# Router comparisons in PSUM, another layout of the left tile pool, and gated products written in w2's row order, in a two-layer encoder kernel

## The chip, the cores and the metric

The kernel runs on one core of one Trainium2 chip. The metric is the device time of one execution in microseconds, from the first to the last instruction and what lies around it, with all inputs in DRAM as float32.

## What is computed

Two encoder layers run over 256 tokens of width 1024. Each has a token mixer and a mixture of experts, and after each of them stands a LayerNorm over a scaled residual. Cut to what matters here:

```
for l in range(DEPTH):                                   # DEPTH = 2
    mix = mixer(h, w_in[l], ..., w_out[l])               # attention, window attention, gated delta rule
    h = layernorm(ALPHA * h + mix, ln1_g[l], ln1_b[l])
    s = sigmoid(h @ w_router)                            # 32 experts, 8 groups of 4
    sel = s + router_bias
    # group score = sum of a group's two best sel; the best group; in it the two best experts
    # comb[token, e] = s of a chosen expert / sum of the two, 0 elsewhere
    y = sum(comb[:, e:e+1] * ((silu(h @ w1[l][e]) * (h @ w3[l][e])) @ w2[l][e]) for e in range(32))
    h = layernorm(ALPHA * h + y, ln2_g[l], ln2_b[l])
```

w1 and w3 are 1024 x 512 and w2 is 512 x 1024 for each expert, so a layer reads 192 slabs of 1 MB for its experts.

## The kernel before

**Layers.** `mixer(l)` runs first, then `moe(l)`. Two pools of SBUF tiles stand against each other: the right one holds a ring of NR = 15 places of 8 KB a partition, the left one is opened anew for each mixer (`open_mixer`) and for each mixture of experts. A tile in a newly opened left pool waits for the last reader or writer of whatever lay in the same bytes before.

**Weights of the experts.** `fetcher(l)` lists the 192 slabs (`todo`) in the order of use and issues them on SP's DMA queue, which is in order: a load that waits for its place holds up all loads behind it. The places are the ring of 15 on the right and NL = 7 on the left (`wl0` to `wl6`), used in turn. One more place on the left, `op`, takes the very first slab of expert 0, and later the results of the experts (`ops`), which `combine` reads for the last time in the last matmuls of the layer. So 23 slabs can lie in SBUF before PE has used any, and the 24th needs the place of the second slab in use.

**Router.** `project` ends the mixer: it projects, forms the residual, and computes logits from the transposed h (`hx`, in the bytes of the tile `gc`) before the norm is applied. `moe` then chooses experts on DVE with tensors of 16 to 256 elements a partition. `s` is the sigmoid, `sel` adds the bias, `hi`, `lo`, `m1`, `ml` and `gs` give the group scores, `d8` and `d4` are all pairwise differences of groups and of experts in a group, `ge` and `loss` count who beats whom, and `both` is the choice. PE turns it into ranks (`rk`), DVE into positions (`pos`) and one-hot matrices `P`, with which PE gathers 64 tokens for each expert (`gather`, line 1448 copies them out of PSUM). Beside this chain ACT and POOL split h into an upper part `hh` (ACT casts) and a remainder `hl` (POOL subtractions), which `gather` multiplies by `P`.

**Experts.** For each expert `up` makes 64 matmuls, ACT the tanh (line 1473), DVE two products into `hid`, PE two transposes (`transpose_hid`), ACT a copy to `hidT`, and `down` 16 matmuls. `expert_step(e)` issues up(e), then combine and transposes of P, then down(e - 1), gathers for a later expert, and only then the transposes of hid(e).

**Between the layers.** Layer 2 begins on SP's queue with the two vectors of the closing LayerNorm, broadcast to 128 partitions into `gains` (lines 1574 and 1575), and behind them stand all its weights of the mixer. ACT and DVE cut the first of these weights (`uh`, `ul`) ahead of the norm's statistics (line 235). `gains` lies 20,640 bytes after the pool's start, and so did the place `op`.

Of the kernel before, what the change touches and what calls it, by code (L numbers as in the profile page):

```python
# [113 lines left out]
def kernel(ctx: ExitStack, tc: tile.TileContext, a: dict, out: bass.AP):  # L114
# [1170 lines left out]
    def moe(l, fetch, slab, reserve):  # L1285
        P, W, X, PT, ops, hid, hidT = {}, {}, {}, {}, {}, {}, {}
# [52 lines left out]
        sm = rt[:, 128:].rearrange("p (a b) -> p a b", a=10)  # L1339
        hi, lo = (sm[:, 2 * i:2 * i + 2].rearrange("p a b -> p (a b)").rearrange("p (x c) -> p x c", c=2)  # L1340
                  for i in range(2))
        m1, ml, gs, ge = (sm[:, 4 + i] for i in range(4))
        r2 = sm[:, 8]
# [287 lines left out]
```

## Time and profile before

| | |
|---|---|
| device time, median of 3 runs | 1470.63 us (1470.15 to 1471.12) |
| the profiled execution's own time | 1470.02 us |
| its span, first to last instruction | 1468.4 us |
| busy share of the span: PE, DVE, ACT, POOL | 91%, 43%, 28%, 18% |
| mean DMA rate over the span | 327 GB/s |
| mean granted clock of PE | 0.972 of full speed |

The span falls into two equal halves of a mixer, a router and 32 experts. All rows below come from the profiled execution; a start in a timeline counts from its first instruction. PE is TensorE's matmuls, DVE VectorE, ACT ScalarE, POOL GpSimd, SP the engine that issues most transfers. A bracket at the end of a timeline row gives the idle time before it and what ended that.

### The profile page before, as it was taken

Reading aid. Unit: us, or ns where it says so; the run is one execution under the profiler, and the core shown is the slowest. Engines: PE = TensorE matmul, PEld = TensorE weight load, DVE = VectorE, ACT = ScalarE, POOL = GpSimd, SP = SyncE. Lnnn points to the kernel's source line nnn. Section 1 sums busy time; section 2 is a strip of 40 time slices with the busy share of each in tenths; the row PEclk is TensorE's granted clock in tenths of the full one; section 3 lists DMA queues with packets and bytes.
Section 4 is the critical chain, followed back from the end, with each engine's and each line's share of the span. In section 5 each row is a group of like instructions: output and inputs, shape, how many; then the busy total and the mean of one; then the engine's idle time right before and its main releaser. Section 6 shows DMA issues by size and latency. Waiting matters only on the chain. (4 is left out here: it accounts for less than half of the span.)

```text
span 1468.4 us, 23692 instructions
## 1 busy us (share of the span) xinstructions
PE 1341.5 (91%) x9708; PEld 893.4 (61%) x9708; DVE 632.3 (43%) x1214; ACT 403.8 (28%) x769; POOL 266.2 (18%) x327
## 2 busy tenths in 40 slices
PE   6889999799998999999678799997999899999986
PEld 5768777555554555555367677774555556555542
DVE  6887667622221222222169875775222212222213
ACT  3445543211111111211134455332211111111111
POOL 4485304300000000000036743033000000000000
PEclk9999999899999999999979899999999999999999
DMA  7535779699999999999655457796999999999995
GB/s 232 168 123 148 226 244 344 233 405 419 419 419 417 419 419 419 419 419 420 266 163 156 138 141 255 242 355 239 407 418 419 418 418 419 420 419 419 419 419 212
DMA packets 114533, 479.89 MB, mean 327 GB/s; under 512 B 25168, under 2 KB 38000, under 8 KB 65520
## 3 DMA queue, kind: packets, MB, share of 16 engines
q1 hardware_dynamic: 112464, 471.85, 82.7%
q0 software_dynamic: 1376, 5.24, 1.0%
q8 instruction: 81, 1.33, 0.4%
q10 hardware_dynamic: 576, 1.18, 0.2%
q14 instruction: 36, 0.29, 0.1%
HBM read 476.40 MB, written 1.84 MB: 326 GB/s over the span
## 5 line engine op out<-in xcount | busy, mean ns | idle before, releaser
L176 PE MATMUL h<-w,h 128*64 128x256 f32 x2016 | 232.7, 387 | 21.7 <-PEq L1382 9.5
L176 PEld LDWEIGHTS h<-w,h 128*64 128x64 f32 x2016 | 144.0, 139 | 100.3 <-issue 16.6
L170 DVE SCALAR_TENSOR_TENSOR hid<-hid,h 128x256 f32<-128x256 f32 x64 | 27.0, 421 | 401.3 <-ACT hid L1473 401.3
L170 DVE SCALAR_TENSOR_TENSOR op<-mo,rt,op 64x512 fp32r<-64x512 f32 x128 | 95.9, 749 | 223.0 <-ACT op L1500 222.0
L1500 ACT ACTIVATE op<-mo,rt 64x512 fp32r<-64x512 f32 x128 | 87.4, 683 | 314.5 <-PE mo L176 275.1
L176 PE MATMUL mo<-w,hidT 128*64 128x512 f32 x720 | 164.3, 595 | 3.5 <-DMA w<-in_w_dram 2.2
L161 POOL TENSOR_TENSOR W<-P,rt 128x128 f32<-128x128 f32 x64 | 24.2, 399 | 785.2 <-PE PT L182 710.3
L1473 ACT ACTIVATE hid<-h 128x256 f32<-128x256 f32 x64 | 24.6, 385 | 402.3 <-PE h L176 402.3
L176 PEld LDWEIGHTS mo<-w,hidT 128*64 128x64 f32 x720 | 50.7, 137 | 89.1 <-issue 77.3
L176 PE MATMUL h<-w,xg 128*64 128x256 f32 x864 | 96.9, 380 | 2.3 <-ACT h L1448 2.3
L176 PE MATMUL h<-wl,h 128*64 128x256 f32 x768 | 86.3, 381 | 2.1 <-ACT h L1448 1.4
L176 PEld LDWEIGHTS h<-w,xg 128*64 128x64 f32 x864 | 61.0, 137 | 33.6 <-ACT h L1448 3.4
L176 PE MATMUL mo<-wl,hidT 128*64 128x512 f32 x304 | 69.8, 597 | 2.5 <-DMA wl<-in_w_dram 2.5
L176 PEld LDWEIGHTS h<-wl,h 128*64 128x64 f32 x768 | 53.9, 137 | 29.9 <-ACT h L1448 2.1
L176 PE MATMUL my<-op,PT 128*128 128x512 f32 x256 | 69.7, 412 | 2.1 <-ACT op L1500 1.4
L176 PE MATMUL xg<-P,hh 128*128 128x256 f32 x256 | 56.4, 303 | 5.8 <-DVE P L161 5.8
L176 PEld LDWEIGHTS my<-op,PT 128*128 128x128 f32 x256 | 45.5, 188 | 25.4 <-issue 11.5
L176 PEld LDWEIGHTS xg<-P,hh 128*128 128x128 f32 x256 | 40.8, 196 | 29.6 <-issue 29.5
L176 PE MATMUL xg<-P,hl 128*128 128x256 f32 x256 | 52.7, 288 | 0.0
L176 PE MATMUL h<-wl,xg 128*64 128x256 f32 x416 | 47.7, 382 | 3.2 <-DMA wl<-in_w_dram 1.6
L176 PEld LDWEIGHTS mo<-wl,hidT 128*64 128x64 f32 x304 | 20.6, 137 | 37.3 <-issue 29.8
L176 PE MATMUL wo<-uh_wo,ym 128*128 128x512 f32 x128 | 41.4, 395 | 0.0
(436 smaller groups left out, 2463.9 us busy)
## 6 DMA issues: line engine op xcount, KB each, us to landing
w<-in_w_dram SPq DMA_DIRECT2D x268, 1024.0 KB, 19.9
wl<-in_w_dram SPq DMA_DIRECT2D x112, 1024.0 KB, 19.9
w_gb<-in_w_in_dram SPq DMA_DIRECT2D x16, 512.0 KB, 3.7
w_gc<-in_w_in_dram SPq DMA_DIRECT2D x16, 512.0 KB, 4.5
w_wo<-in_w_out_dram SPq DMA_DIRECT2D x16, 512.0 KB, 4.8
w_ga<-in_w_in_dram SPq DMA_DIRECT2D x14, 512.0 KB, 4.7
w_cqk<-in_w_in_dram SPq DMA_DIRECT2D x8, 512.0 KB, 3.7
w_aq<-in_w_in_dram SPq DMA_DIRECT2D x8, 512.0 KB, 4.5
```

The lines of the kernel that those rows point to most:

```text
L161: return eng.tensor_tensor(out=o, in0=x, in1=y, op=op).ins
L170: return V.scalar_tensor_tensor(out=o, in0=x, scalar=s, in1=y, op0=op0, op1=op1)
L176: ins = T.matmul(o, l, r, start=start, stop=stop, skip_group_check=True).ins
L1473: A.activation(u, b[:, :256], AF.Tanh, scale=0.5)
L1500: A.activation(hi, src, AF.Copy, scale=w)
```

## The change

**Choice of experts.** The tiles of the choice (`s`, `sel`, `hi`, `lo`, `m1`, `gs`, `d8`, `d4`, `loss`) lie in two PSUM banks, `ch` and `d4`. Where an operation takes two tensors, one comes from PSUM and the other from SBUF, for which `sel` and `gs` are computed twice (`sel2`, `gs2` in the SBUF tile `gate`). The pair sums and maxima become reductions. The positions are made in PSUM too (`first`); `P` reads them there, and ACT copies them to `pos`.

**Left pool.** A pad of 128 bytes comes first, so `hh` covers exactly the bytes of `gc`; before, it took in the last 128 bytes of `mix`, the LayerNorm's vectors that POOL reads last. The places `op` and `wl0` change sides, so that `gains` of the next layer lies on `wl0` and `op` on the mixer's `ym0`. The first slab is loaded as the 19th instead of the 16th. h is split token half by token half instead of column half by column half.

**Products.** tanh goes into a tile of its own, `gate`, and the two products read every second element and write `hid` in halves, which the transposes then read without a stride.

```diff
+FIRST = 18
...
                 stt(m1[:, 3:4], m1[:, 0:1], -1.0, m1[:, 2:3], OP.mult, OP.mult)
-                shifted(1, 0, mix[:, 1], m1)
                 logits(1, 1)
                 folded = scaled(1, m1)
+                shifted(1, 0, mix[:, 1], m1)
...
-        todo.insert(NR, todo.pop(0))
+        todo.insert(FIRST, todo.pop(0))
...
-                j = (i if i < NR else i - 1) % (NR + NL) - NR
-                if i == NR:
+                j = (i if i < FIRST else i - 1) % (NR + NL) - NR
+                if i == FIRST:
                     w = lefts.pop("op", None) or left("op")
...
+               "gate": lambda e: st((128, 256), "gate", f"gate{l}{e}"),
...
+        scope["pad"] = st((128, 32), "pad", f"pad{l}")
         X[2] = st((128, 8, 2, 64), "xg", f"xg{l}2")
         W[0], PT[0], P[0] = (new[n](0) for n in ("W", "PT", "P"))
 
         part_h = lambda n: st((128, 2, 8, 128), n, f"{n}{l}", dt=F32R)
         hs = [part_h("hh")]
-        rt = st((128, 288), "rt", f"rt{l}")
-
-        scratch = [st((128, n), x, f"rs{x}{l}") for x, n in (("hid", 256), ("hidT", 256), ("sc", 128))]
+        rt = st((128, 192), "rt", f"rt{l}")
+        both = st((128, 128), "both", f"both{l}", dt=BF16)[:, :64].rearrange("p (t e) -> p t e", t=2)
+        gate[0], hid[0], hidT[0] = (new[n](0) for n in ("gate", "hid", "hidT"))
         fl = st((128, 1), "fl", f"fl{l}", dt=I32)
-        scope["pad"] = st((128, 128), "pad", f"pad{l}")
-        reserve(("op", 0, 1, 2))
+        reserve((0, "op", 1, 2))
         hs.append(part_h("hl"))
         reserve((3, 4, 5, 6))
...
-        for j in range(2):
-            for t in range(2):
+        for t in range(2):
+            for j in range(2):
                 k = slice(4 * j, 4 * j + 4)
                 split(hs[0][:, t, k], hs[1][:, t, k], hv[:, t, k], G)
...
-        s, sel, loss = (scratch[0][:, 64 * i:64 * i + 64].rearrange("p (t e) -> p t e", t=2) for i in range(3))
-        both = scratch[0][:, 192:224].bitcast(BF16).rearrange("p (t e) -> p t e", t=2)
-        d4 = scratch[1].rearrange("p (g i j) -> p g i j", i=4, j=4)
-        d8 = scratch[2].rearrange("p (t i j) -> p t i j", i=8, j=8)
...
+        ch, d4 = bank("s", f"ch{l}"), bank("s", f"d4{l}")[:, :256].rearrange("p (g i j) -> p g i j", i=4, j=4)
+        s, sel, loss = (ch[:, 64 * i:64 * i + 64].rearrange("p (t e) -> p t e", t=2) for i in range(3))
+        d8 = ch[:, 192:320].rearrange("p (t i j) -> p t i j", i=8, j=8)
+        hi, lo = (ch[:, 320 + 32 * i:352 + 32 * i] for i in range(2))
+        m1, gs = (ch[:, 384 + 16 * i:400 + 16 * i] for i in range(2))
+        sel2 = gate[0][:, :64].rearrange("p (t e) -> p t e", t=2)
+        ml, gs2, ge = (gate[0][:, 64 + 16 * i:80 + 16 * i] for i in range(3))
...
-        tt(V, sel, s, rbias[:, None, :].to_broadcast([128, 2, NE]), OP.add)
+        for o in (sel, sel2):
+            tt(V, o, s, rbias[:, None, :].to_broadcast([128, 2, NE]), OP.add)
...
-        tt(V, hi, gv[:, :, 0::2], gv[:, :, 1::2], OP.max)
-        tt(V, lo, gv[:, :, 0::2], gv[:, :, 1::2], OP.add)
-        tt(V, m1, hi[:, :, 0], hi[:, :, 1], OP.add)
-        tt(V, ml, lo[:, :, 0], lo[:, :, 1], OP.max)
-        tt(V, gs, m1, ml, OP.max)
-        tt(V, d4, *pairs(gv, 4), OP.subtract)
-        tt(V, d8, *pairs(gs.rearrange("p (t g) -> p t g", t=2), 8), OP.subtract)
+        for o, op in ((hi, OP.max), (lo, OP.add)):
+            V.tensor_reduce(out=o, in_=sel2.rearrange("p t (x j) -> p (t x) j", j=2), axis=AX.X, op=op)
+        V.tensor_reduce(out=m1, in_=hi.rearrange("p (x c) -> p x c", c=2), axis=AX.X, op=OP.add)
+        V.tensor_reduce(out=ml, in_=lo.rearrange("p (x c) -> p x c", c=2), axis=AX.X, op=OP.max)
+        for o in (gs, gs2):
+            tt(V, o, m1, ml, OP.max)
...
+        against(d8, by_8(gs), by_8(gs2), 8)
+        against(d4, by_4(sel), by_4(sel2), 4)
...
-        stt(pos, rkv, 1.0, both, OP.add, OP.mult)
+        stt(first, rkv, 1.0, both, OP.add, OP.mult)
...
-            u = hid[e] = hid.get(e) or new["hid"](e)
-            A.activation(u, b[:, :256], AF.Tanh, scale=0.5)
-            stt(u, u, 1.0, b[:, :256], OP.add, OP.mult)
-            scope["last"] = [tt(V, u, u, b[:, 256:], OP.mult)]
+            g, u = (x.get(e) or new[n](e) for n, x in (("gate", gate), ("hid", hid)))
+            hid[e] = u
+            A.activation(g, b[:, :256], AF.Tanh, scale=0.5)
+
+            rows = lambda ap: ap.rearrange("s (p j) -> s j p", j=2)
+            uv = u.rearrange("s (j p) -> s j p", j=2)
+            stt(uv, rows(g), 1.0, rows(b[:, :256]), OP.add, OP.mult)
+            scope["last"] = [tt(V, uv, uv, rows(b[:, 256:]), OP.mult)]
...
-                tp(b[:, j * 128:(j + 1) * 128], hid[e][:, j::2])
+                tp(b[:, j * 128:(j + 1) * 128], hid[e][:, j * 128:(j + 1) * 128])
...
-            select(0)
+            select(0, first)
+            A.copy(pos, first)
...
-        scope["stats"] = [sm[:, t] for t in range(2)]
+        scope["stats"] = [sm[:, 2 + t] for t in range(2)]
```

On DVE, in layer 1's choice of experts (all names with `rs` are SBUF tiles of the choice, `rk` is a PSUM bank, `cst` holds constants), there stood, from the differences of experts to the one-hot matrices:

```order
L161 TENSOR_TENSOR rshidT_2710<-rshid_2709 128x256
L161 TENSOR_TENSOR rt_2708<-rt_2708 128x16 x3
L161 TENSOR_TENSOR rssc_2711<-rt_2708 128x128
L161 TENSOR_TENSOR rssc_2711<-rssc_2711,cst 128x128
L161 TENSOR_TENSOR rshidT_2710<-rshidT_2710,cst 128x256
L1363 TENSOR_REDUCE rt_2708<-rssc_2711 128x16
L1366 TENSOR_REDUCE rshid_2709<-rshidT_2710 128x64
L170 SCALAR_TENSOR_TENSOR rshid_2709<-rshid_2709,rt_2708 128x64
L161 TENSOR_TENSOR rt_2708<-rshid_2709 128x64
L170 SCALAR_TENSOR_TENSOR rt_2708<-rk_2765,rshid_2709 128x64
L1536 TENSOR_REDUCE rt_2708<-rt_2708 128x2
L161 TENSOR_TENSOR P_2706<-rt_2708,cst 128x256 x2
```

and now stands (`ch` and `d` are PSUM banks, `gate` and `both` SBUF tiles):

```order
L162 TENSOR_TENSOR gate_2711<-ch_2750,gate_2711 128x16
L162 TENSOR_TENSOR ch_2750<-ch_2750,gate_2711 128x128
L162 TENSOR_TENSOR d_2751<-ch_2750,gate_2711 128x256
L162 TENSOR_TENSOR ch_2750<-ch_2750,cst 128x128
L162 TENSOR_TENSOR d_2751<-d_2751,cst 128x256
L1371 TENSOR_REDUCE gate_2711<-ch_2750 128x16
L1374 TENSOR_REDUCE ch_2750<-d_2751 128x64
L171 SCALAR_TENSOR_TENSOR both_2710<-ch_2750,gate_2711 128x64
L162 TENSOR_TENSOR rt_2709<-ch_2750,both_2710 128x64
L171 SCALAR_TENSOR_TENSOR rk_2770<-rk_2770,both_2710 128x64
L1548 TENSOR_REDUCE rt_2709<-rt_2709 128x2
L162 TENSOR_TENSOR P_2707<-rk_2770,cst 128x256 x2
```

The differences of groups come first, no row shown has two inputs in SBUF, and P reads the positions in the bank `rk`.

On SP, where the last places before layer 1's experts are filled (`w` is a place of the ring, `wl` one on the left, `wl0op` the first slab), there stood:

```order
L1272 DMA w_2541<-in_w_dram 128x2048
L1272 DMA w_2696<-in_w_dram 128x2048
L1272 DMA wl0op_2714<-in_w_dram 128x2048
L1272 DMA wl_2715<-in_w_dram 128x2048
L1272 DMA wl_2716<-in_w_dram 128x2048
L1272 DMA wl_2717<-in_w_dram 128x2048
```

and now:

```order
L1273 DMA w_2541<-in_w_dram 128x2048
L1273 DMA w_2696<-in_w_dram 128x2048
L1273 DMA wl_2715<-in_w_dram 128x2048
L1273 DMA wl_2717<-in_w_dram 128x2048
L1273 DMA wl_2718<-in_w_dram 128x2048
L1273 DMA wl0op_2716<-in_w_dram 128x2048
```

The first slab's load has moved behind three others.

On SP, at the end of layer 1 (with what each row waits for: `DMAHW` other transfers, `PE` and `DVE` those engines), there stood:

```order
L1272 DMA w_5827<-in_w_dram 128x1024 [waits DMAHW1_49]
L1574 DMA gains_5858<-in_ln_g_dram 128x1024 [waits DMAHW2_49,DVE_49,PE_49]
L1575 DMA gains_5858<-in_ln_b_dram 128x1024 [waits DMAHW3_49]
L275 DMA w_5860<-in_w_in_dram 128x2x512 [waits DMAHW4_49]
```

and now:

```order
L1273 DMA w_5862<-in_w_dram 128x1024 [waits DMAHW1_49]
L1586 DMA gains_5893<-in_ln_g_dram 128x1024 [waits DMAHW2_49,PE_49]
L1587 DMA gains_5893<-in_ln_b_dram 128x1024 [waits DMAHW3_49]
L276 DMA w_5895<-in_w_in_dram 128x2x512 [waits DMAHW4_49,PE_49]
```

The order is the same; the load of `gains` no longer waits for DVE, and its wait for PE is now for a slab on the left, not for the layer's last matmuls.

## Rows read from the trace of the kernel before

**Rows 1.** Busy time by stretch: engines (instructions), PE clock, DMA share, GB/s.

```profile
264.00:287.50 23.50, 15.72 (x105) 9.74 (x105) 16.30 (x40) 7.13 (x12) 11.30 (x11) 0.78 0.47 183
287.50:718.50 431.00, 413.31 (x2965) 240.92 (x2966) 100.58 (x198) 72.40 (x154) 10.57 (x28) 0.99 1.00 412
718.50:742.60 24.10, 6.67 (x26) 3.01 (x26) 10.15 (x13) 7.11 (x9) 5.74 (x7) 0.78 0.52 176
```

**Rows 2.** Timeline of SP's DMA issues: start, time, line, destination, count.

```profile
287.51 29.39 SPq L1272 DMA_DIRECT2D w<-in_w_dram  x15
691.72 10.26 SPq L1272 DMA_DIRECT2D w<-in_w_dram  x5
726.89 0.33 SPq L1574 DMA_DIRECT2D gains<-in_ln_g_dram  x1
1016.04 29.39 SPq L1272 DMA_DIRECT2D w<-in_w_dram  x15
```

**Rows 3.** PE timeline, layer 1, first gather, first slabs, second gather, first transposes.

```profile
278.75 0.89 PE L176 MATMUL xg<-P,hh 128*128 128x256 f32 x2 [2.92 <-DVE P L161]
...
282.98 2.75 PE L176 MATMUL h<-wl0op,h 128*64 128x256 f32 x16
...
287.39 0.51 PE L176 MATMUL xg<-P,hh 128*128 128x256 f32 x2
...
289.48 3.67 PE L176 MATMUL h<-w,h 128*64 128x256 f32 x32
294.64 0.48 PE L182 MATMUL hT<-cst,hid 128*128 128x128 f32 x2 [1.49 <-DVE hid L161]
```

**Rows 4.** PE timeline, layer 2, the first gather's first matmuls.

```profile
1008.59 0.89 PE L176 MATMUL xg<-P,hh 128*128 128x256 f32 x2 [2.91 <-DVE P L161]
```

**Rows 5.** DVE timeline, layer 1, router chain; the last row is undisturbed, later.

```profile
268.23 0.33 DVE L165 TENSOR_SCALAR rshid<-lg 128x32 f32<-128x32 f32 x2
...
269.60 1.38 DVE L161 TENSOR_TENSOR rt<-rshid 128x32 f32<-128x32 f32 x2
...
272.26 1.74 DVE L161 TENSOR_TENSOR rshidT<-rshidT,cst 128x256 f32<-128x256 f32 x1
...
275.50 1.44 DVE L161 TENSOR_TENSOR rt<-rshid 128x64 f32<-128x64 f32 x1
276.86 0.21 DVE L170 SCALAR_TENSOR_TENSOR rt<-rk,rshid 128x64 f32<-128x64 f32 x1
...
277.17 1.77 DVE L161 TENSOR_TENSOR P<-rt,cst 128x256 fp32r<-128x256 f32 x2
...
289.93 0.75 DVE L161 TENSOR_TENSOR P<-rt,cst 128x256 fp32r<-128x256 f32 x2
```

**Rows 6.** POOL timeline, layer 1, beside that chain.

```profile
268.22 2.61 POOL L161 TENSOR_TENSOR h<-h,mix 128x512 f32<-128x512 f32 x2 [1.12 <-ACT h L1220]
272.06 6.26 POOL L186 TENSOR_TENSOR hl<-h,hh 128x512 fp32r<-128x512 f32 x4 [1.23 <-DVE rssc L161]
```

**Rows 7.** DVE groups by form, one operand in PSUM: count, busy us, mean ns.

```profile
L170 DVE SCALAR_TENSOR_TENSOR hid<-hid,h 128x256 f32<-128x256 f32 x64 | 27.0, 421 | 401.3 <-ACT hid L1473 401.3
...
L170 DVE SCALAR_TENSOR_TENSOR lg<-lg,stats,bwr 128x32 f32<-128x32 f32 x4 | 1.0, 254 | 0.0
```

**Rows 8.** PE timeline between the layers: last matmuls of layer 1, first after.

```profile
724.64 2.22 PE L176 MATMUL my<-op,PT 128*128 128x512 f32 x7 [0.28 <-DVE op L170]
742.61 1.94 PE L182 MATMUL tp<-cst,h 128*128 128x128 f32 x8 [15.75 <-DVE h L170]
```

**Rows 9.** ACT timeline: a strided cast in layer 1, then the layers' boundary.

```profile
270.86 4.17 ACT L186 CAST hh<-h 128x512 fp32r<-128x512 f32 x4 [2.52 <-POOL h L161]
...
723.12 1.39 ACT L1500 ACTIVATE op<-mo,rt 64x512 fp32r<-64x512 f32 x2 [2.50 <-PE mo L176]
734.27 1.04 ACT L186 CAST uh<-w 128x1024 fp32r<-128x1024 f32 x1 [9.76 <-DMA w<-in_w_in_dram]
```

**Rows 10.** DVE timeline at the boundary: the next layer's first statistics.

```profile
736.60 1.30 DVE L235 BATCH_NORM_STATS2 stats<-my 128x6 f32<-128x512 f32 x2
```

More of the change, by code (lines that the diff above doesn't have):

```diff
@@ L1277, in slab @@
             at[0] += 1
-            while len(got) <= max(i, NR):
+            while len(got) <= max(i, FIRST):
                 fetch(i + 1)
-            return got[NR if i == 0 else i - 1 if i <= NR else i]
+            return got[FIRST if i == 0 else i - 1 if i <= FIRST else i]
         return fetch, slab, lambda js: lefts.update((j, left(j)) for j in js)
     def moe(l, fetch, slab, reserve):
-        P, W, X, PT, ops, hid, hidT = {}, {}, {}, {}, {}, {}, {}
+        P, W, X, PT, ops, gate, hid, hidT = {}, {}, {}, {}, {}, {}, {}, {}
         new = {"P": lambda q: st((128, 2, 4, 64), "P", f"P{l}{q}", dt=F32R),
@@ L1334, in moe @@
         comb, pos = (rt[:, 64 * i:64 * i + 64].rearrange("p (t e) -> p t e", t=2) for i in range(2))
-        s, sel, loss = (scratch[0][:, 64 * i:64 * i + 64].rearrange("p (t e) -> p t e", t=2) for i in range(3))
-        both = scratch[0][:, 192:224].bitcast(BF16).rearrange("p (t e) -> p t e", t=2)
-        d4 = scratch[1].rearrange("p (g i j) -> p g i j", i=4, j=4)
-        d8 = scratch[2].rearrange("p (t i j) -> p t i j", i=8, j=8)
[L1339 to L1343, printed above, removed]
+        ch, d4 = bank("s", f"ch{l}"), bank("s", f"d4{l}")[:, :256].rearrange("p (g i j) -> p g i j", i=4, j=4)
[5 more added lines that the diff above has]
+        ml, gs2, ge = (gate[0][:, 64 + 16 * i:80 + 16 * i] for i in range(3))
+        sm = rt[:, 128:].rearrange("p (a b) -> p a b", a=4)
+        r2, over = sm[:, 0], sm[:, 1, 0:1]
         slotw = r2[:, 12:14]
@@ L1347, in moe, with against @@
         V.reciprocal(s, s)
-        tt(V, sel, s, rbias[:, None, :].to_broadcast([128, 2, NE]), OP.add)
-        gv = sel.rearrange("p t (g c) -> p (t g) c", c=4)
-        pairs = lambda ap, n: (ap[:, :, None, :].to_broadcast([128, ap.shape[1], n, n]),
-                               ap[:, :, :, None].to_broadcast([128, ap.shape[1], n, n]))
-        tie = lambda d, n: C("tie").rearrange("p (i j) -> p i j", j=8)[:, None, :n, :n].to_broadcast([128, d.shape[1], n, n])
-        tt(V, hi, gv[:, :, 0::2], gv[:, :, 1::2], OP.max)
-        tt(V, lo, gv[:, :, 0::2], gv[:, :, 1::2], OP.add)
-        tt(V, m1, hi[:, :, 0], hi[:, :, 1], OP.add)
-        tt(V, ml, lo[:, :, 0], lo[:, :, 1], OP.max)
-        tt(V, gs, m1, ml, OP.max)
-        tt(V, d4, *pairs(gv, 4), OP.subtract)
-        tt(V, d8, *pairs(gs.rearrange("p (t g) -> p t g", t=2), 8), OP.subtract)
+        for o in (sel, sel2):
+            tt(V, o, s, rbias[:, None, :].to_broadcast([128, 2, NE]), OP.add)
+        def against(o, x, y, n):
+            to = [128, o.shape[1], n, n]
+            return tt(V, o, x[:, :, None, :].to_broadcast(to), y[:, :, :, None].to_broadcast(to), OP.subtract)
+        tie = lambda d, n: C("tie").rearrange("p (i j) -> p i j", j=8)[:, None, :n, :n].to_broadcast([128, d.shape[1], n, n])
+        for o, op in ((hi, OP.max), (lo, OP.add)):
[4 more added lines that the diff above has]
+            tt(V, o, m1, ml, OP.max)
+        by_4, by_8 = (lambda ap: ap.rearrange("p t (g c) -> p (t g) c", c=4)), (lambda ap: ap.rearrange("p (t g) -> p t g", t=2))
+        against(d8, by_8(gs), by_8(gs2), 8)
+        against(d4, by_4(sel), by_4(sel2), 4)
         beaten = tt(V, d8, d8, tie(d8, 8), OP.is_ge)
-        V.tensor_reduce(out=ge.rearrange("p (t g) -> p t g", t=2), in_=d8, axis=AX.X, op=OP.max)
+        V.tensor_reduce(out=by_8(ge), in_=d8, axis=AX.X, op=OP.max)
         with tc.issue_after(beaten):
@@ L1374, in moe @@
         ranked = mm(b[:, 64:96], ones, both[:, 1], False, True)
-        rkv = b[:, 0:64].rearrange("p (t e) -> p t e", t=2)
-        stt(pos, rkv, 1.0, both, OP.add, OP.mult)
+        rkv, first = (b[:, i:i + 64].rearrange("p (t e) -> p t e", t=2) for i in (0, 96))
+        stt(first, rkv, 1.0, both, OP.add, OP.mult)
         pin.__exit__(None, None, None)
@@ L1385, in general @@
                 u = st((128, 256), "hid", f"ou{l}")
-                over = sm[:, 9, 0:1]
                 with tc.For_i(0, NE) as e:
@@ L1415, in general, with select @@
                                    part("w2", 8 * half + i), False, False)
-        def select(q):
+        def select(q, pos=pos):
             P[q] = P.get(q) or new["P"](q)
```

## The prediction

> **What bounds the kernel now.** I read the busy time by stretch first. In the 431 us of layer 1's experts the DMA share is 1.00 at 412 GB/s; around it lie two short stretches in which neither PE nor the DMA engines are full: 264.0 to 287.5 us (DMA 0.47, PE busy 15.7 of 23.5 us, clock 0.78) and 718.5 to 742.6 us (DMA 0.52, PE 6.7 of 24.1 us) [rows 1]. A change on DVE or ACT inside the 431 us is worth nothing while the transfers are the limit; the stretches around it are worth their full length.
>
> SP's issues show why the first stretch counts. The 24th slab is issued at 287.51 us in layer 1 and at 1016.04 us in layer 2 [rows 2], when PE has finished the second slab. From there on each slab follows the one before at the DMA rate, and PE keeps up; so whatever makes PE finish the second slab earlier moves the end of the layer by the same amount. PE's rows go back from there: two slabs from 282.98, the first gather from 278.75, and that gather had waited for P on DVE [rows 3]. Layer 2 has the same wait, gathering from 1008.59 [rows 4].
>
> The second stretch is the boundary of the layers. PE's last matmuls end at 724.64 + 2.22 = 726.86, and the next begin at 742.61, 15.75 us later, after the norm [rows 8]. SP issues the norm's `gains` only at 726.89, and the mixer's weights stand behind it in the queue [rows 2]. ACT's first cast of these weights waits for the transfer until 734.27 [rows 9], and the statistics of the norm, behind DVE's part of that cut, start at 736.60 [rows 10], 9.7 us after PE was done with the numbers they read.
>
> **Boundary: the place of `gains`.** Now its load waits for a slab on the left that was read some twenty slabs earlier, no longer for the layer's last matmuls. It can be issued behind the last experts' slabs: five go out from 691.72 on in 10.26 us [rows 2], the last at about 702 and 2.5 us apart, so at that step the first six loads of layer 2 are in the queue by about 717. What is late next is ACT, which finishes the last results at 723.12 + 1.39 = 724.51 [rows 9]; the cast can then follow at once if the weight is there. From cast to statistics took 736.60 - 734.27 = 2.33 us [rows 9, 10], so the statistics start at 726.84, just as PE ends: 9.7 us gained. The doubt is the landing. Before, the weight was usable 734.27 - 726.89 = 7.4 us after the first issue [rows 2, 9]. If the whole 7.4 us began only at 718.5, where the experts' stretch ends, the cast would start at 725.9 and the gain would be 8.4. As the transfers overlap the last slabs I take nearer the upper end, **9.4 us**. POOL's and DVE's cuts of the other first weights shift with it, and so does every later load, since each waits for a cut.
>
> **Router chain, twice.** DVE's chain starts at 268.23 and P begins at 277.17 and ends at 278.94 [rows 5]. POOL works beside it from 268.22 to 270.83 and from 272.06 to 278.32 [rows 6]. DVE operations with two inputs in SBUF are stretched there: the 128x256 comparison takes 1.74 us, the 128x64 product 1.44, the two P 1.77, where two P without POOL beside them take 0.75 [rows 5]. The position step, with one input in PSUM, takes 0.21 in the middle of POOL's run [rows 5]. So one input in PSUM escapes the wait. Operations with one PSUM operand cost 0.25 us for 32 elements and 0.42 for 256 [rows 7].
>
> The new chain up to the choice has 18 operations. It starts 0.2 us later, at 268.45, since the norm's `shifted` now stands ahead. I cost it so: the two first ones 0.33 together [rows 5], and by these two prices (0.25 at 16 to 64 elements, 0.42 at 256, the line between for 128) ten small ones at 0.2 to 0.25, two of 128 at 0.3, two of 256 at 0.42 and two counting reductions at 0.3 and 0.4, together 4.9, and 0.5 for the steps between them. It ends near 273.9, where the old one ended near 275.5 with the 1.44 us product following it [rows 5]. The bounds: 0.8 us better if the small ones are as short as the 0.21 row and the steps overlap, and no gain in this part if each of the 18 costs 0.1 more because of PSUM. Behind it stand the ranks on PE (an estimate of 0.5, with the weighted choice on DVE beside them, no longer 1.44), the positions (0.21), a sum (0.2) and two P at 0.42 each [rows 5, 7]. P ends at about 275.7, against 278.94: **3.2 us** earlier.
>
> Three things hang on it. `hl`: the first gather now needs POOL's third subtraction, since the halves go token by token. But `hh` no longer waits for POOL's last read of `mix`, so ACT can start at about 268.4, not 270.86 [rows 9], and POOL at 270.9, not 272.06; at 6.26 / 4 = 1.57 us each [rows 6] the third ends at 275.6, level with P. No cost, but POOL would be next if DVE were faster. Second, the copy of the positions on ACT: ACT is free from about 273 to the first gather's copy, so nothing. Third, the first slab's later load: it is the 19th of 23, and the DMA share of 0.47 [rows 1] says that all 23 have landed after some 11 of the 23.5 us, so nothing; if it came last it would still be there.
>
> **Strided products.** 64 pairs of products of 0.42 us each [rows 7] now read every second element. ACT's strided cast of 512 elements takes 4.17 / 4 = 1.04 us, as much as a contiguous one of 1024 [rows 9]. The price thus lies between nothing and a doubling, 0.84 us for a pair. It is covered by `down` of the expert before, which stands between up and the transposes, except for expert 0, where PE waited 1.49 us for hid [rows 3]. I take 0.3 us for each layer. Contiguous reads in the transposes gain nothing that a DMA-bound stretch could show.
>
> The Trainium skill, page "SBUF — State Buffer", section "Door 1: The DMA port swizzle", says that accesses that leave a line of 16 bytes (8 in PSUM) pay a penalty, so that the stride costs most for the operand in PSUM. No row here shows a product with that stride; with a full doubling by that rule the sum would be 1.1 us worse, an estimate.
>
> The Trainium skill's page "VectorE: DVE Perf Modes", section "Why PSUM operands drop a tier", speaks against the move itself: a PSUM operand keeps float32 at one element a cycle, while single-input operations in SBUF may run at two. By it the few single-input steps of the chain would lose at most 0.3 us in a layer, an estimate, and the sum would be 0.6 us worse.
>
> **The clock.** PE's granted clock averages 0.78 in 264 to 287.5 us [rows 1]; at its lower level the first gather with the two transposes of W behind it took 282.98 - 278.75 = 4.2 us, where the second gather, without such transposes, took 2.1 [rows 3]: the factor between 1.2 and 2.4 GHz. PE still idles over 3 us ahead of the gather, so I let the clock fall as before. The second slab ended 8.8 us after the gather's start in layer 1 and 7.5 in layer 2 [rows 2 to 4]; I keep the sum of the two.
>
> **Sum.** 9.4 + 2 x (3.2 - 0.3) = 15.2 us. The profiled execution took 1470.02 us, so 1454.8; the median of the runs is 0.6 above it: **1455.4 us**, 1.0% faster. Differences under 0.2% (2.9 us) are about what a measurement of this kernel cannot tell from no change.
>
> **Rivals.**
> - *The boundary alone gains.* PSUM writes make the chain as long as it was, or POOL's `hl` comes later and the gather waits for it. Then 9.4 - 0.6 = 8.8 us, 1461.8. For it: no row shows a chain of DVE operations from PSUM to PSUM. Against it: the stretched rows alone hold 1.0 + 1.2 + 1.3 us of waiting [rows 5].
> - *The clock stays up in the gather.* With the idle time halved, PE gathers at 2.4 GHz: 2.1 us, 0.4 for the transposes and 3.67 for two slabs [rows 3], 6.2 in place of 8.8 and 7.5. That is 3.9 us more in all, 1451.5. Against it: 3 us of idle time remain.
> - *The router alone gains.* Loads of layer 2 land late, because they share the DMA engines with the last slabs and hold those up: the boundary gains only 2 to 4 us, 1461 to 1463.
> - *Slower.* The strided products outgrow their cover. Between up(e) and the transposes of hid(e) lie 16 matmuls with the columns of 32 of `up`, which take 3.67 us [rows 3]; a tanh as long as a product needs 0.4 of that. The pair would have to take more than 3.25 us, nearly four times 0.84, before PE waited, and then each 0.1 us costs up to 6.2 us over 62 experts; from 3.5 us on the kernel is slower than before, with a pair of 3.6 us about 1477. The nearest strided row shows a factor of two.
> - *The change does not reach the path*, because another wait (the flag, the copy of the positions) ends where P ended: within 0.2%, 1470.
>
> Chances: the forecast (1453 to 1459) 0.58, boundary alone 0.15, clock up 0.14, router alone 0.07, no effect 0.03, slower 0.03. The range from 1450 to 1462 takes in the first three. Faster 0.94, same 0.03, slower 0.03.
>
> **What would show it.** SP's issue of `gains` at about 705 us instead of 726.89; ACT's cast near 722 to 725 in time, right behind the last results; the statistics less than 1 us after PE's last matmul. P ending some 7.3 us after the chain's start instead of 10.7, no DVE row of the choice above 0.6 us, the next slab issued about 3 us earlier against the logits in each layer. The experts' stretches keep 431 us at full DMA share. Wrong would be a gather that starts after P and behind POOL, a PSUM row at twice its price, or a boundary where ACT still waits for a transfer.

## The result, and the profile after

The changed kernel takes 1453.11 us (median of 4 runs, 1452.09 to 1454.18) against 1470.63: a ratio of 0.9878 (95% interval 0.9864 to 0.9891), 1.2% faster. The forecast was 1455.4, in a range from 1450 to 1462. The profiled execution took 1453.74 us, span 1452.1 us; before it was 1470.02 and 1468.4.

Busy time by stretch of the changed kernel, with the same columns and bounds moved along, answers to [rows 1]:

```profile
264.00:283.10 19.10, 15.02 (x91) 9.41 (x88) 12.72 (x41) 7.27 (x13) 11.02 (x11) 0.82 0.57 222
283.10:715.00 431.90, 412.15 (x2965) 240.17 (x2966) 100.54 (x198) 72.30 (x153) 10.57 (x28) 0.99 1.01 414
715.00:729.50 14.50, 6.76 (x27) 3.02 (x26) 10.10 (x13) 7.17 (x9) 5.74 (x7) 0.93 0.62 215
```

The two short stretches shrank, 23.5 to 19.1 us and 24.1 to 14.5; between them lies the stretch at full DMA share, nearly as long as before (431.9 us, 431.0 then). SP's queue shows the same two gains (answer to [rows 2]):

```profile
283.13 29.26 SPq L1273 DMA_DIRECT2D w<-in_w_dram  x15
...
702.21 0.33 SPq L1586 DMA_DIRECT2D gains<-in_ln_g_dram  x1
...
709.69 5.33 SPq L276 DMA_DIRECT2D w_ga<-in_w_in_dram  x3
...
999.78 29.27 SPq L1273 DMA_DIRECT2D w<-in_w_dram  x15
```

The 24th slab goes out at 283.13 in place of 287.51, in layer 2 at 999.78 in place of 1016.04, and the gains at 702.21 in place of 726.89, with the loads of layer 2 behind them.

PE's timeline around the first gather (answer to [rows 3, 4]); the last column is idle time before a row and what ended it:

```profile
274.32 0.88 PE L177 MATMUL xg<-P,hh 128*128 128x256 f32 x2 [0.94 <-DVE P L162]
275.00 0.63 PE L177 MATMUL xg<-P,hl 128*128 128x256 f32 x2
...
277.99 0.63 PE L183 MATMUL PT<-cst,W 128*128 128x128 f32 x2
278.55 2.81 PE L177 MATMUL h<-wl0op,h 128*64 128x256 f32 x16
281.19 1.89 PE L177 MATMUL h<-w,h 128*64 128x256 f32 x16
...
283.36 0.40 PE L177 MATMUL xg<-P,hl 128*128 128x256 f32 x2
```

The gather starts at 274.32 and still waits for P. Its first row takes 0.88 us and those behind it 0.63 us for two matmuls, where the second gather takes 0.40: it runs at the lower clock, as before. DVE's chain, which answers to [rows 5]:

```profile
267.64 0.50 DVE L166 TENSOR_SCALAR ch<-lg 128x32 f32<-128x32 f32 x2
268.17 0.56 DVE L1350 RECIPROCAL ch<-ch 128x64 f32<-128x64 f32 x1
...
270.28 0.18 DVE L162 TENSOR_TENSOR ch<-ch,gate 128x16 f32<-128x16 f32 x1
270.50 0.17 DVE L162 TENSOR_TENSOR gate<-ch,gate 128x16 f32<-128x16 f32 x1
270.70 0.30 DVE L162 TENSOR_TENSOR ch<-ch,gate 128x128 f32<-128x128 f32 x1
271.04 0.43 DVE L162 TENSOR_TENSOR d<-ch,gate 128x256 f32<-128x256 f32 x1
...
271.71 0.42 DVE L162 TENSOR_TENSOR d<-d,cst 128x256 f32<-128x256 f32 x1
...
272.82 0.22 DVE L171 SCALAR_TENSOR_TENSOR both<-ch,gate 128x64 bf16<-128x64 f32 x1
...
273.75 0.76 DVE L162 TENSOR_TENSOR P<-rk,cst 128x256 fp32r<-128x256 f32 x2
...
274.61 1.58 DVE L162 TENSOR_TENSOR rt<-rt 128x64 f32<-128x64 f32 x1
```

Nothing in it takes more than 0.56 us up to P. The comparison of 128x256 elements fell from 1.74 to 0.42 us and the two P from 1.77 to 0.76 us. One row is long, the product at 274.61 (1.58 us): its two inputs lie in SBUF, and POOL is still running. POOL and ACT beside it (answers to [rows 6, 9]):

```profile
267.53 2.68 POOL L162 TENSOR_TENSOR h<-h,mix 128x512 f32<-128x512 f32 x2 [1.12 <-ACT lg L1184]
270.16 5.95 POOL L187 TENSOR_TENSOR hl<-h,hh 128x512 fp32r<-128x512 f32 x4
```

```profile
267.43 2.15 ACT L187 CAST hh<-h 128x512 fp32r<-128x512 f32 x2
```

ACT's first two casts `hh` no longer wait for POOL at 267.43, and POOL's third `hl` ends at 270.16 + 3/4 x 5.95 = 274.62, 0.11 us after P's end (274.51). Last the boundary: PE, ACT and DVE (answers to [rows 8 to 10]):

```profile
721.29 2.22 PE L177 MATMUL my<-op,PT 128*128 128x512 f32 x7 [0.29 <-DVE op L171]
729.55 1.94 PE L183 MATMUL tp<-cst,h 128*128 128x128 f32 x8 [6.04 <-DVE h L171]
```

```profile
719.77 1.39 ACT L1511 ACTIVATE op<-mo,rt 64x512 fp32r<-64x512 f32 x2 [2.50 <-PE mo L177]
721.22 1.05 ACT L187 CAST uh<-w 128x1024 fp32r<-128x1024 f32 x1
```

```profile
722.30 1.22 DVE L187 TENSOR_TENSOR ul<-w,uh 128x1024 fp32r<-128x1024 f32 x1 [0.28 <-ACT uh L187]
723.55 1.29 DVE L236 BATCH_NORM_STATS2 stats<-my 128x6 f32<-128x512 f32 x2
...
726.58 3.48 DVE L171 SCALAR_TENSOR_TENSOR h<-h,stats,gains 128x512 f32<-128x512 f32 x2
```

The cast of layer 2's first weights starts 0.06 us after ACT's last results end (719.77 + 1.39 = 721.16), and the statistics at 723.55, 0.04 us after PE's last matmul (721.29 + 2.22 = 723.51). PE idles 6.04 us in place of 15.75.

### The profile page after: what moved, and what is told of

Same layout as the page of the kernel before. It is cut to its first block, busy times and chain, and to the rows that moved or that the text cites. A ratio compares the mean times of both kernels' runs of the same rounds, so it can differ in the third digit from the quotient of the medians.

```text
span 1452.1 us, 23761 instructions
## 1 busy us (share of the span) xinstructions
PE 1340.0 (92%) x9708; PEld 892.1 (61%) x9708; DVE 626.2 (43%) x1218; ACT 404.1 (28%) x771; POOL 263.9 (18%) x327
## 5 line engine op out<-in xcount | busy, mean ns | idle before, releaser
L171 DVE SCALAR_TENSOR_TENSOR hid<-gate,h 128x256 f32<-128x256 f32 x64 | 26.9, 421 | 405.3 <-ACT gate L1481 405.3
L1481 ACT ACTIVATE gate<-h 128x256 f32<-128x256 f32 x64 | 24.5, 384 | 406.3 <-PE h L177 406.3
```

Of the source, the lines that this page charges most:

```text
L171: return V.scalar_tensor_tensor(out=o, in0=x, scalar=s, in1=y, op0=op0, op1=op1)
L1481: A.activation(g, b[:, :256], AF.Tanh, scale=0.5)
```

## The experiments

Each kernel ran in turns with the kernel before, the first four of the table on one chip, the next four on a second, the last four on a third. The kernel before had medians of 1469.75, 1468.86 and 1469.65 us there. after_again is the changed kernel once more. The times:

| kernel | median us | ratio to the kernel before, 95% interval |
|---|---|---|
| boundary_alone | 1461.33 | 0.9942 (0.9928 to 0.9955) |
| router_alone | 1462.05 | 0.9951 (0.9937 to 0.9964) |
| choice_in_sbuf | 1461.18 | 0.9947 (0.9933 to 0.9960) |
| pe_kept_busy | 1450.94 | 0.9876 (0.9861 to 0.9891) |
| after_again | 1453.25 | 0.9889 (0.9872 to 0.9905) |
| pe_kept_busy_full | 1450.15 | 0.9872 (0.9855 to 0.9888) |
| hh_over_mix | 1455.56 | 0.9905 (0.9888 to 0.9921) |
| old_product_order | 1452.95 | 0.9891 (0.9875 to 0.9908) |
| boundary_filled | 1452.09 | 0.9882 (0.9866 to 0.9899) |
| pe_busy_transposes_later | 1448.84 | 0.9859 (0.9839 to 0.9880) |
| all_three | 1449.11 | 0.9863 (0.9846 to 0.9879) |
| first_fifteen | 1451.88 | 0.9879 (0.9862 to 0.9895) |

Whole times differ by a microsecond or two between executions of one kernel: layer 1's mixer, the same code in all of them, ends between 266.0 and 267.9 us. So I read three distances inside each trace. The first is from the start of PE's last logits row (`lg<-gap`) to that of the first gather row (`xg<-P,hh`), for the router's chain. The second is from there to SP's issue of the 24th slab (for after, 283.13 - 274.32 = 8.81). The third is from PE's last `my` to the first `tp` between the layers. All in us, layer 1 / layer 2:

| kernel | logits to gather | gather to 24th slab | between the layers |
|---|---|---|---|
| before | 11.69 / 11.70 | 8.76 / 7.45 | 15.75 |
| after | 7.95 / 7.96 | 8.81 / 8.94 | 6.04 |
| after_again | 7.98 / 7.96 | 8.36 / 8.89 | 6.05 |
| boundary_alone | 11.68 / 11.69 | 8.72 / 8.83 | 6.03 |
| router_alone | 7.98 / 7.96 | 8.41 / 7.44 | 15.78 |
| choice_in_sbuf | 12.42 / 12.41 | 7.90 / 8.24 | 6.06 |
| hh_over_mix | 7.96 / 7.96 | 9.54 / 9.48 | 6.03 |
| old_product_order | 7.96 / 7.97 | 8.72 / 7.36 | 6.06 |
| pe_kept_busy | 7.97 / 7.96 | 7.07 / 7.07 | 6.05 |
| pe_kept_busy_full | 7.96 / 7.97 | 7.06 / 7.07 | 6.05 |
| boundary_filled | 7.97 / 7.96 | 8.31 / 7.56 | 5.95 |
| pe_busy_transposes_later | 7.96 / 7.96 | 6.46 / 6.43 | 6.05 |
| all_three | 7.95 / 7.96 | 6.43 / 6.43 | 5.98 |
| first_fifteen | 7.96 / 7.96 | 7.61 / 8.73 | 6.07 |

### The two parts apart

boundary_alone is the kernel before with this edit and the index `FIRST` in the fetcher; router_alone is the changed kernel with both lines set back:

```diff
+FIRST = 18
-        reserve(("op", 0, 1, 2))
+        reserve((0, "op", 1, 2))
```

> Kernel before, with only the places on the left and the step of the first slab's load taken from the change. Theory (the two parts of the change add up, since a transfer-bound stretch lies between them): the statistics of the norm between the layers start as PE's last matmul ends, 9.7 us earlier, the router's chain stays as it was: 1470.6 - 9.7 = 1460.9 us. Rival (the boundary's gain is partly given back by the loads that now share the DMA engines with the last slabs, and the router's part brought more): 1463 to 1465. Rival (most of the 17.5 us came from the boundary): 1456 or less.

> Changed kernel, with the left places and the first slab's load as in the kernel before. Theory: SP issues the gains only when PE is done, the statistics start 9.7 us later than in the changed kernel, and the router's part stays: 1453.1 + 9.7 = 1462.8 us. Rival (the router's shorter chain is worth little, the slabs are held back by the transfers anyway): 1468 to 1470. With the run of the boundary alone: the two gains should sum to 17.5 us; a sum well above or below says that one part gives something back to the other.

The boundary alone brings 1469.75 - 1461.33 = 8.4 us, the router alone 7.7 us, together 16.1; the whole change brought 17.5 beside one set of runs and 15.6 beside another (after_again). The distances separate cleanly: boundary_alone has the short boundary and the long chain, router_alone the reverse. The 8.4 is less than the 9.7 between PE's rows at the boundary: in boundary_alone's profile the two stretches from the gather to the 24th slab took 1.3 us more than in the profile of before, though the edit doesn't touch their code. PE's rows between the layers in router_alone:

```profile
720.21 2.21 PE L177 MATMUL my<-op,PT 128*128 128x512 f32 x7 [0.29 <-DVE op L171]
738.20 1.94 PE L183 MATMUL tp<-cst,h 128*128 128x128 f32 x8 [15.78 <-DVE h L171]
```

So the parts add up, and neither hangs on the other. The "router worth little" and "most of it from the boundary" rivals are out.

first_fifteen keeps the new places and sets only the step of the load back (`FIRST = 15`):

> Changed kernel, with the first slab's load at the 16th step again, the places on the left as in the changed kernel. Theory (the place of gains brings the gain between the layers, not the step of the load): the first slab's load now waits for the place that lies between that of gains and the units, it may be issued some microseconds later, but all slabs have landed long before the first gather: within 1 us of 1453.2. Rival (the order of the loads matters, since the slabs behind it in the queue are issued later): 1 to 3 us slower.

1451.88 us, and the boundary is 6.07 us. SP issues the first slab's load at 251.84 in place of 254.57, the last of the eight on the left goes out at about 266 us in both, and from its issue to its first use the slab has 27 us with this edit and 24 in the changed kernel. The place brings the boundary's gain; the step of the load brings nothing that shows.

### The place of the choice: PSUM or SBUF

```diff
-        ch, d4 = bank("s", f"ch{l}"), bank("s", f"d4{l}")[:, :256].rearrange("p (g i j) -> p g i j", i=4, j=4)
-        s, sel, loss = (ch[:, 64 * i:64 * i + 64].rearrange("p (t e) -> p t e", t=2) for i in range(3))
-        d8 = ch[:, 192:320].rearrange("p (t i j) -> p t i j", i=8, j=8)
-        hi, lo = (ch[:, 320 + 32 * i:352 + 32 * i] for i in range(2))
-        m1, gs = (ch[:, 384 + 16 * i:400 + 16 * i] for i in range(2))
+        d4 = hidT[0].rearrange("p a b -> p (a b)").rearrange("p (g i j) -> p g i j", i=4, j=4)
+        s, sel = (hid[0][:, 64 * i:64 * i + 64].rearrange("p (t e) -> p t e", t=2) for i in range(2))
+        loss = gate[0][:, 112:176].rearrange("p (t e) -> p t e", t=2)
+        d8 = hid[0][:, 128:256].rearrange("p (t i j) -> p t i j", i=8, j=8)
+        hi, lo = (gate[0][:, 112 + 32 * i:144 + 32 * i] for i in range(2))
+        m1, gs = (gate[0][:, 176 + 16 * i:192 + 16 * i] for i in range(2))
```

> Changed kernel, with the tiles of the choice of experts in SBUF in place of PSUM; the same operations in the same order, and the places of hh, of hl and of the slabs unchanged. Theory (operations with two inputs in SBUF wait for POOL's running instruction): several rows of the chain grow from 0.2-0.4 us to 1.0-1.8 us, the first gather starts 2.5 to 3.5 us later in each layer: 1458 to 1460 us. Rival (the chain became shorter through hh's earlier start and the rebuilt steps, not through the place of its tiles): rows stay below 0.6 us, 1453 to 1454.

It took 1461.18 us: the router's whole gain is gone and a little more. DVE's rows, the same operations, though the differences of experts (`hidT<-hid,gate`) now come ahead of those of groups:

```profile
267.68 0.28 DVE L166 TENSOR_SCALAR hid<-lg 128x32 f32<-128x32 f32 x2
...
269.51 1.01 DVE L162 TENSOR_TENSOR hidT<-hid,gate 128x256 f32<-128x256 f32 x1
...
270.66 1.38 DVE L162 TENSOR_TENSOR gate<-gate 128x16 f32<-128x16 f32 x2
272.07 1.50 DVE L162 TENSOR_TENSOR hid<-gate 128x128 f32<-128x128 f32 x1
273.60 1.48 DVE L162 TENSOR_TENSOR hid<-hid,cst 128x128 f32<-128x128 f32 x1
275.00 1.73 DVE L162 TENSOR_TENSOR hidT<-hidT,cst 128x256 f32<-128x256 f32 x1
```

Two operations on 16 elements took 1.38 us together; they took 0.18 and 0.17 in PSUM. The 128-element steps took 1.50 and 1.48 (0.30), the 256-element ones 1.01 and 1.73 (0.43 and 0.42). POOL was at work beside all of these rows, from 270.21 to 276.45 us with its four `hl`, 1.56 us each here (1.49 in the changed kernel). After that, at 279.12, the 64-element product `rt<-rt` with both inputs in SBUF took 0.22 us, where it took 1.58 beside POOL in the changed kernel. Steps with one input went the other way: the nine of the choice take 2.65 us in the changed kernel and 2.19 here, the first two 0.50 and 0.28. The first gather came 4.46 us later against the logits, more than the 2.5 to 3.5 I had put down, because I had counted the rows that were stretched before and not the small ones that the rebuilt chain adds. So the move into PSUM carries the router's gain; the earlier `hh` and the rebuilt steps without it lost 0.7 us (12.42 against 11.69). The two other reorderings, the cut of h by token halves and the norm's `shifted` ahead of the choice, were not run alone. The Trainium skill, page "SBUF — State Buffer", section "Who interferes with whom", says that a VectorE instruction with two SBUF inputs contends with a GpSimd instruction that reads SBUF, and that one with at most one SBUF input, outside the modes that use two ports, does not. The rows here agree: 1.38 us against 0.35 for the same pair of steps.

### POOL's `hl`: how near it is to the path

The 128 bytes ahead of `X[2]` and `hh` go behind them:

```diff
-        scope["pad"] = st((128, 32), "pad", f"pad{l}")
...
         fl = st((128, 1), "fl", f"fl{l}", dt=I32)
+        scope["pad"] = st((128, 32), "pad", f"pad{l}")
```

> Changed kernel, with hh moved down by 128 bytes on the left, so that it overlaps the end of mix again as in the kernel before. Theory (the free start of hh keeps POOL's hl off the path): ACT's first hh starts only when POOL has read mix, 2.7 us later, POOL's third hl ends 1.1 us later, behind P, and the first gather's matmuls on hl wait for it: 0.7 to 1.1 us a layer, 1.5 to 2.2 us in all. Rival (POOL's cut has more than a microsecond of slack, since the gather begins with hh): no change.

1455.56 us, 2.3 above the changed kernel on the same chip. ACT, POOL and PE:

```profile
270.99 4.19 ACT L187 CAST hh<-h 128x512 fp32r<-128x512 f32 x4 [2.69 <-POOL h L162]
```

```profile
272.19 5.97 POOL L187 TENSOR_TENSOR hl<-h,hh 128x512 fp32r<-128x512 f32 x4 [1.23 <-ACT hh L187]
```

```profile
275.09 0.88 PE L177 MATMUL xg<-P,hh 128*128 128x256 f32 x2 [0.94 <-DVE P L162]
...
276.71 0.58 PE L177 MATMUL xg<-P,hl 128*128 128x256 f32 x1 [0.52 <-POOL hl L187]
```

The gather still starts 7.96 us after the logits, but its matmul on `hl` for the second half of the tokens waits 0.52 us for POOL. The next matmuls on `hh` start 1.99 us after the gather's start (277.08) in place of 1.11 (275.43 in the changed kernel), 0.88 later, within the 0.7 to 1.1 expected, and the 24th slab is issued 9.5 us after the gather's start in both layers. So the early start of `hh`, which hangs on 128 bytes of padding, is part of the gain: without it the faster chain runs into POOL's cut.

### The order of the gated products

```diff
-            stt(uv, rows(g), 1.0, rows(b[:, :256]), OP.add, OP.mult)
-            scope["last"] = [tt(V, uv, uv, rows(b[:, 256:]), OP.mult)]
+            stt(u, g, 1.0, b[:, :256], OP.add, OP.mult)
+            scope["last"] = [tt(V, u, u, b[:, 256:], OP.mult)]
-                tp(b[:, j * 128:(j + 1) * 128], hid[e][:, j * 128:(j + 1) * 128])
+                tp(b[:, j * 128:(j + 1) * 128], hid[e][:, j::2])
```

> Changed kernel, with the gated products written in the order of their columns again and the transposes reading every second element, as in the kernel before. Theory (a stride of two elements costs DVE nothing here): the two products stay at 0.42 us each, PE's wait for hid at expert 0 stays near 1.5 us, the transposes of hid take up to 0.07 us more each, all of it hidden by the transfers: within 1 us of the changed kernel. Rival (the estimate on record, 0.3 us a layer for the stride): the products are shorter by 0.1 to 0.4 us, the time 0.6 us lower.

1452.95 against 1453.25 us. DVE's groups by form, count, busy us and mean ns, first of the changed kernel, then of this one:

```profile
L171 DVE SCALAR_TENSOR_TENSOR hid<-gate,h 128x256 f32<-128x256 f32 x64 | 26.9, 421 | 405.3 <-ACT gate L1481 405.3
L162 DVE TENSOR_TENSOR hid<-hid,h 128x256 f32<-128x256 f32 x64 | 26.9, 420 | 2.2
```

```profile
L171 DVE SCALAR_TENSOR_TENSOR hid<-gate,h 128x256 f32<-128x256 f32 x64 | 27.0, 421 | 406.3 <-ACT gate L1481 406.3
L162 DVE TENSOR_TENSOR hid<-hid,h 128x256 f32<-128x256 f32 x64 | 26.9, 420 | 2.2
```

421 and 420 ns with the stride and without it. In the changed kernel the first product reads both its inputs at a step of two elements, the second one its input in PSUM; the outputs are written without a step. That stride cost nothing here, so the 0.3 us a layer put down for it was not there.

### The clock in the gather

Two kernels fill PE's idle time ahead of the gather by repeating starts, the matmuls that put h into the sums `yb`. The edit shown is that of pe_kept_busy_full, with three whole starts; in pe_kept_busy the first and the last of the three are matmuls of 256 columns (`mm(yb[0][0][:, :256], ident, h[:, 0, :256], True, False)`):

```diff
             start(1, 0)
+            start(0, 0)
             start(1, 1)
+            start(1, 1)
...
+        start(1, 1)
         stt(first, rkv, 1.0, both, OP.add, OP.mult)
```

> Changed kernel, with four more matmuls in each layer that repeat the start of the sums yb in PE's idle time ahead of the first gather (they write the same numbers once more). Theory (the granted clock falls because PE idles 1.7 and 0.9 us ahead of the gather): the first gather and the two transposes run at 2.4 GHz, the second slab ends 6.3 us after the gather's start in place of 8.8 and 8.9, 5.1 us in two layers: 1448 us. Rival (the clock is down for another reason than these idle times): the rows of the gather stay at 0.63 us for two matmuls, 1453, or up to 1 us more where a repeated start stands ahead of the ranks.

> The changed kernel itself, unaltered, so that the runs beside it have it on the same chip: 1452 to 1453 us, ratio to the kernel before 0.987 to 0.989.

> Changed kernel, with three more matmuls of 512 columns in each layer that repeat whole starts of the sums yb in PE's idle time ahead of the first gather; the result is unaffected. Theory (idle time ahead of the gather lets the granted clock fall): the gather's matmuls take 0.40 us for two in place of 0.63, the second slab ends 7.1 us after the gather's start as in the run with half starts, in place of 8.8 and 8.9; W on POOL is what PE waits for next; 3.5 us less than the changed kernel in the same call. Rival (what the run with half starts gained is given back elsewhere, or was the difference between two executions): within 1 us of the changed kernel.

The half starts do change the sums `yb` after all, so that kernel's time counts for the placing of the matmuls alone. The whole starts leave `yb` as it is: 1450.15 us, all four runs (1448.97 to 1451.52) below those of the changed kernel beside them (1451.72 to 1453.86), and 1.30 and 1.82 us less from the gather to the 24th slab. Stretches with the granted clock, ahead of the gather and in it, first of the changed kernel, then with the whole starts:

```profile
268.00:274.30 6.30, 2.83 (x11) 0.94 (x10) 5.68 (x22) 3.74 (x4) 6.22 (x5) 0.94 1.00 421
274.30:278.50 4.20, 4.18 (x18) 3.88 (x18) 2.84 (x8) 0.58 (x2) 2.57 (x4) 0.50 0.23 98
```

```profile
268.00:274.70 6.70, 5.84 (x18) 2.08 (x16) 5.97 (x24) 4.16 (x4) 6.62 (x5) 1.00 1.00 422
274.70:278.00 3.30, 2.90 (x19) 2.31 (x18) 2.93 (x8) 0.79 (x3) 2.67 (x4) 1.00 0.30 124
```

A granted clock of 0.50 is 1.2 GHz, 1.00 is 2.4. With PE busy 5.84 us ahead of the gather in place of 2.83 it does not fall there. What PE waits for next is POOL's W:

```profile
274.73 0.69 PE L177 MATMUL xg<-P,hh 128*128 128x256 f32 x2
275.26 0.40 PE L177 MATMUL xg<-P,hl 128*128 128x256 f32 x2
...
277.46 0.68 PE L183 MATMUL PT<-cst,W 128*128 128x128 f32 x2 [0.37 <-POOL W L162]
278.08 1.95 PE L177 MATMUL h<-wl0op,h 128*64 128x256 f32 x16
```

That wait and the two transposes go behind the second slab in the next kernel:

```diff
-            transpose_P(0)
...
                     gather(0, 6)
+                    transpose_P(0)
```

> The kernel with PE kept busy ahead of the gather (1450.15 us), with the two transposes of W for the first pair of experts moved behind the second slab. Theory (they and PE's wait for W on POOL, 0.4 + 0.6 us, lie on the path to the second slab's end, on which SP's next load hangs): the second slab ends about 0.6 to 1.0 us earlier against the gather's start, 6.1 to 6.5 us in place of 7.1; 1448 to 1449 us. Rival (the first slab now waits for the gather's last copies on DVE and ACT for as long as the transposes took): no change, 1450.

The 24th slab goes out 6.43 to 6.46 us after the gather's start, 0.6 earlier in each layer; a wait of 0.41 us for the gather's last copy on DVE took back the rest. 1448.84 us is 1.3 us below the 1450.15 on the other chip, which the spread of the runs (1446.83 to 1451.6) does not settle.

### The clock between the layers

```diff
+            if l == 0:
+                b = bank("s", f"idle{l}")
+                for _ in range(12):
+                    mm(b[:, :256], ident, cst[:, :256], True, True)
```

> Changed kernel, with twelve matmuls of 256 columns on constants in PE's 6.0 us of idle time between the layers; nothing reads what they write. Theory (the idle time lets the granted clock fall for the first 4.6 us of layer 2): the eight transposes of the norm's result take about 1.0 us in place of 1.94 and the first ga matmuls 0.39 in place of 0.63 for one, up to 2.3 us less: 1451 us. Rival (PE there waits for the cuts of the weights, so that a faster PE only idles more): the rows of PE are shorter and the time is within 1 us of 1453.2.

> Changed kernel, with PE kept busy ahead of the gather in both layers, PE kept busy between the layers, and the first transposes of W behind the second slab. Theory: the three gains add, 3.1 + 2 + 1.5: 1446 to 1447 us, faster than both kernels. Rival (what the clock gives at the boundary is lost in the mixer, which is held by the cuts and not by PE): 1448 to 1449.

PE between the layers in boundary_filled:

```profile
721.60 5.34 PE L177 MATMUL idle<-cst 128*128 128x256 f32 x24
727.71 1.32 PE L183 MATMUL tp<-cst,h 128*128 128x128 f32 x8 [0.77 <-DVE h L171]
...
731.14 0.40 PE L177 MATMUL ga<-uh_ga,placeT 128*128 128x512 f32 x1
```

The clock stays at 1.00 (0.56 in the changed kernel from 729.5 to 735) and the rows are shorter: the second set of transposes starts 735.24 - 727.71 = 7.53 us after the first, in the changed kernel 738.27 - 729.55 = 8.72 (8.13 to 9.14 in all kernels with its boundary and no fill). From there the lead is lost: from the first `tp` to layer 2's last logits row it is 253.39 us, 253.33 in the changed kernel. In all_three it is 251.28, but from 252.38 to 253.99 in the kernels that have the changed kernel's boundary. The times say no more: 1452.09 against 1453.11 and 1453.25 on other chips and 1451.88 on the same chip (first_fifteen, the changed kernel but for the step of one load), and all_three at 1449.11 against 1448.84 without this fill. Whether the fill is worth up to a microsecond or nothing stays open. All four runs of all_three (1447.38 to 1450.04) and three of the four of pe_busy_transposes_later (1446.83 to 1449.27, the fourth 1451.6) lie below those of first_fifteen (1451.54 to 1452.62); which of the two is better these runs don't tell.

## Why the prediction was right, point by point

The median came out 2.3 us below the forecast of 1455.4, at the lower edge of the 1453 to 1459 that the forecast kept for itself, and nearer to the 1451.5 of the rival in which the clock stays up. The time alone doesn't choose between the two; the gather's rows at 0.63 us do. The medians moved by 17.5 us, and by 15.6 beside after_again, so a microsecond or two belongs to the runs and not to the kernel; the account below is of the two profiled executions.

The profiled spans differ by 1468.4 - 1452.1 = 16.3 us. The traces split it so: boundary 15.75 - 6.04 = 9.7; logits to gather 2 x 3.74 = 7.5; gather to the 24th slab 16.2 - 17.8 = -1.5; and, in stretches that the change doesn't touch, layer 1's mixer 0.7 and layer 2's 1.0 faster, layer 1's transfer-bound stretch (24th slab to the last `my`'s end, 439.35 and 440.38) 1.0 slower. That sums to 16.3. The terms of the forecast, 15.2 in all, against these:

- **Boundary, 9.4: it was 9.7.** The loads were in the queue by 715 (709.69 + 5.33, the third of the `w_ga`), and no transfer was waited for at the first cast. The doubt about the landing, 8.4, did not come true.
- **Router chain, 3.2 a layer: it was 3.74.** The chain to the choice took 5.4 us (267.64 to 273.04), as costed (4.9 + 0.5). What was too dear stood behind it: ranks, positions, sum and P took 1.47 us (273.04 to 274.51), where 1.8 were put down, and the chain started 0.1 later, not 0.2. The two P overlap, 0.76 together where 2 x 0.42 was taken. Within the chain two errors cancel: the two first steps took 0.50 where 0.33 from SBUF rows was put down, and the steps lay closer together than the 0.5 allowed. The single-input steps lost 0.46 us to PSUM (2.65 against 2.19 in choice_in_sbuf), where the prediction had weighed at most 0.3. The mechanism, one input in PSUM, is shown by choice_in_sbuf.
- **POOL level with P: so it was,** 274.62 and 274.51, and hh_over_mix shows what it costs to lose that.
- **Strided products, 0.3 a layer: nothing.** By the Trainium skill's page "SBUF — State Buffer", section "Door 1: The DMA port swizzle", which was weighed in the prediction, the stride should have cost most in PSUM (of PSUM the page names only matmuls); here 421 ns stayed 421, and the measurement decides.
- **The clock, kept as before: it fell as before,** but the time it took to come back is no property of the kernel. The prediction read a factor of two from 4.2 and 2.1 us, but the 4.2 hold two transposes more; without them the first gather takes 277.99 - 274.32 = 3.67 us here, 1.75 times the second. The sum over two layers was 16.2 in the profile of before, 17.5 in boundary_alone, which has the same code there, and between 15.85 and 17.75 in the kernels that have the changed code there and no fill. So 1.5 us of the account is the difference of two executions. For the same reason the 24th slab went out 3.7 us earlier against the logits in layer 1 and only 2.2 in layer 2, where about 3 was the sign to look for.

The errors of 0.3, 1.1 and 0.6 us on one side and the clock's 1.5 on the other nearly cancel, which is luck, and the two mixers and the transfers add 0.6. Of the rivals, "the boundary alone gains" fails by router_alone, "the router alone" by boundary_alone, the strided products by the rows above. "The clock stays up" did not happen, and was nevertheless the best lead: made to happen, it gave 3.1 us from the 17.25 that the two stretches take in after_again. The 3.9 forecast for it counts from 16.3, and from there the 14.1 measured are 2.2 (7.07 us to the 24th slab in place of 6.2, with 0.37 of them the wait for W).

## What to carry to other kernels

Where a chain of small VectorE operations runs beside GpSimd on the path, look first at whether both inputs lie in SBUF: putting one of them in PSUM took 4.5 us out of 12.4 here (choice_in_sbuf against the changed kernel). A tile's place on the chip is a wait like any other: ask of each early load which tile it overwrites and who reads that last. Where PE waits ahead of a step that decides, look at its granted clock: harmless matmuls in the idle time were worth 3.1 us of 1453 ahead of the gathers, and nothing that shows between the layers. Ahead of the gathers the next engine that was nearly late, POOL with W, took back 0.37 us.

## What the runs showed of the hardware

- Operations from PSUM to PSUM or with one PSUM input cost as little as 0.17 to 0.23 us for 16 to 64 elements and 0.42 to 0.43 for 256, and a step of two float32 elements in the inputs, the one in PSUM among them, added nothing to 420 ns. Steps with one input were shorter from SBUF to SBUF (0.28 us against 0.50 for two of 32 elements).
- Idle times of 0.82, 1.72 and 0.94 us with a few short matmuls between them brought PE to 1.2 GHz; with the idle times filled it stayed at 2.4. When it came back differed between executions whose code is the same in that stretch: 7.36 to 8.94 us from the gather's start to the 24th slab in the kernels with the changed code there and no fill, 7.06 or 7.07 in all four gathers with PE kept busy and nothing else moved.
- At the boundary DVE's two steps on `h` with two inputs in SBUF take 3.48 us beside POOL (726.58), where the same two for the other half of the tokens, with POOL idle, took 1.41 (735.71). That a PSUM input would shorten PE's 6.0 us of idle time there wasn't tried.
